# Rope: the cosine product from PSUM into a tile of its own

## The chip, the cores and the metric

The kernel runs on one core of one Trainium2 chip. A core has five engines that matter here: TensorE (PE) multiplies matrices into PSUM, VectorE (DVE) and ScalarE (ACT) work on SBUF and PSUM, GpSimd (POOL) works on SBUF, and SyncE (SP) issues the DMAs. Each engine runs its own list of instructions in order and waits on semaphores. The metric is the device time of one execution in microseconds (us), lower is better; a kernel's time is the median of its runs.

## The reference

One hybrid decoder block on a sequence of 1024 tokens of width 1024: an RMS norm, one wide projection, a forgetting attention (eight heads of 64) beside a differential attention (four heads with two 64-wide query and key parts each), SiLU gates, a merge by sigmoid gates, an output projection and a residual. Rope is applied to the queries and keys of the differential branch alone:

```python
def apply_rope(x, cos, sin):
    x1, x2 = jnp.split(x, 2, axis=-1)
    return jnp.concatenate([x1 * c - x2 * s, x2 * c + x1 * s], axis=-1)

qd = apply_rope(qb.reshape(b, s, DIFF_HEADS, 2, DIFF_QK_DIM).transpose(0, 2, 3, 1, 4), cos, sin)
kd = apply_rope(kb.reshape(b, s, DIFF_HEADS, 2, DIFF_QK_DIM).transpose(0, 2, 3, 1, 4), cos, sin)
...
out = (softmax(q1 k1^T) - lam * softmax(q2 k2^T)) v      # causal, per head
```

## The kernel before

The data are fp32. For the multiplications, operands are split into a high part (rounded to the type fp32r) and a low part (the rest), and a product is made of two or three such multiplications.

The kernel has three stages in time. First (to about 110 us) it loads and norms x, transposes it into `hT`, and projects the values (L195). Then (110 to about 555 us) comes the attention: eight units, `u` = 0 to 3 for the differential heads and 4 to 7 for pairs of forgetting heads. Last come the gates, the branch products and the output projection, which PE fills on its own.

In the attention stage, `unit_proj(u)` makes the transposed queries and keys of a unit in four tasks: `k` and `q`, each in two chunks of 512 tokens. A task loads and splits the weights once per kind (`load_w`, L264 on POOL and L266 on DVE), runs 24 matmuls into a PSUM tile of the tag `pj` (`project`, L276), and then, for differential units, calls `rope`; for forgetting units the PSUM tile goes on as it is. `stack` (L325 to L328) then splits the result into high and low halves, two ACT casts and two DVE subtractions. `pj` has two banks, shared with the other projections.

`rope` works on 128 rows: four blocks of 32, and the partner of a row lies in the neighbouring block. ACT copies the PSUM tile to SBUF (`raw`, L313). Four DMAs of 32 rows each (L317) write the blocks in exchanged order into `sw`. DVE multiplies `raw` by the cosines in place (L318), POOL multiplies `sw` by the signed sines (L319), DVE adds the two (L320). The DMAs read `raw`, and L318 overwrites it, so L318 waits for the four DMAs to have landed. There are 16 ropes: four units times q and k times two chunks.

The tiles of the tag `raw` come from three slots. The slots are shared with the spilled projections of `z` (`spill_tasks`, L369 to L371: ACT copy and a DMA to memory) and with the sums of squares of finished heads (`sum_squares`, L378 to L388).

The attention of a unit (`unit_attn`) goes row block by row block: scores into PSUM tiles of the tag `S` (three banks, L429 and L430), a DVE pass that adds the mask, writes the scores to SBUF and finds the row's extreme (L431), exp on ACT (L437), the normalization (L523 to L527), the transposes on PE (L458), their split by ACT (L461) and DVE (L462), and the product with the values (L482). While unit `u` is in its attention, the projections of unit `u + 1` and of `z` are called in between as filler (the loop at L651 to L663), and unit 0 projects before any attention (L627 to L629).

The order of instructions on each engine is not the order of the calls: a planner places them, by the order of the calls as priority and by its own costs of instructions and transfers, and it adds the waits. An engine then runs its list as planned, also when a transfer takes longer than the planner thought.

Of the kernel before, what the change touches and what calls it, by code (L numbers as in the profile page):

```python
# [9 lines left out]
F32 = mybir.dt.float32  # L10
F32R = mybir.dt.float32r
AF = mybir.ActivationFunctionType
ALU = mybir.AluOpType
# [3 lines left out]
P = 128  # L17
# [4 lines left out]
CH = 512  # L22
# [25 lines left out]
def tile_hybrid_block(  # L48
# [18 lines left out]
    nc = tc.nc  # L67
# [187 lines left out]
    def load_w(name, src, hi_act=False, lo_pool=False, pieces=None):  # L255
        raw = wpool.tile([P, KT, P], F32, tag="wraw", name=f"raw_{name}")
        for ks, piece in pieces or [(slice(0, KT), src)]:
            nc.sync.dma_start(raw[:, ks], piece)
        hi = wpool.tile([P, KT, P], F32R, tag="whi", name=f"hi_{name}")
        lo = wpool.tile([P, KT, P], F32R, tag="wlo", name=f"lo_{name}")  # L260
        if hi_act:
            nc.scalar.copy(hi, raw)
        else:
            nc.gpsimd.tensor_scalar(hi, raw, 1.0, 1.0, op0=ALU.mult, op1=ALU.mult)  # L264
        eng = nc.gpsimd if lo_pool else nc.vector
        eng.tensor_tensor(lo, raw, hi, op=ALU.subtract)  # L266
        return hi, lo

    def w_cols(c0):
        return w[:, c0:c0 + P].rearrange("(k p) n -> p k n", p=P)  # L270

    def project(ps, wt, c):
        hi, lo = wt
        for k in range(KT):
            for a, h in ((hi, 0), (hi, 1), (lo, 0)):
                nc.tensor.matmul(  # L276
                    ps, lhsT=a[:, k, :], rhs=hT[h][k // 4][c][:, k % 4, :],
                    start=(k == 0 and a is hi and h == 0), stop=(k == KT - 1 and a is lo))


    with ExitStack() as st:
# [3 lines left out]
        stg = st.enter_context(tc.tile_pool(name="stg", bufs=2, side="right", reuse_waits="tile"))  # L285
# [7 lines left out]
        cosT = big.tile([P, S], F32, tag="big", name="cosT")  # L293
# [7 lines left out]
        def unit_proj(u):  # L301

            diff = u < 4
            t = u if diff else u - 4
            qc, kc = (QB, KB_) if diff else (QA, KA_)
            T = {}
            for n in ("TA", "TB", "KA", "KB"):
                T[n] = qk.tile([P, S], F32R, tag=n, name=f"{n}{u}")

            def rope(ps, c, nm):  # L310
                sl = slice(c * CH, (c + 1) * CH)
                raw = stg.tile([P, CH], F32, tag="raw", name=f"raw{nm}", bufs=3)
                nc.scalar.copy(raw, ps)  # L313
                sw = stg.tile([P, CH], F32, tag="sw", name=f"sw{nm}")
                for b in range(4):
                    o = b ^ 1
                    nc.sync.dma_start(sw[b * 32:(b + 1) * 32, :], raw[o * 32:(o + 1) * 32, :])  # L317
                nc.vector.tensor_tensor(raw, raw, cosT[:, sl], op=ALU.mult)  # L318
                nc.gpsimd.tensor_tensor(sw, sw, sinT[:, sl], op=ALU.mult)  # L319
                nc.vector.tensor_tensor(raw, raw, sw, op=ALU.add)  # L320
                return raw

            def stack(A, B, src, sl):

                nc.scalar.copy(A[UPR, sl], src[UPR])  # L325
                nc.vector.tensor_tensor(A[DNR, sl], src[UPR], A[UPR, sl], op=ALU.subtract)
                nc.scalar.copy(B[DNR, sl], src[DNR])
                nc.vector.tensor_tensor(B[UPR, sl], src[DNR], B[DNR, sl], op=ALU.subtract)  # L328

            def q_chunk(wt, c):  # L330
                sl = slice(c * CH, (c + 1) * CH)
                ps = pj.tile([P, CH], F32, tag="pj", name=f"pq{u}_{c}")
                project(ps, wt, c)
                src = rope(ps, c, f"q{u}_{c}") if diff else ps
                stack(T["TA"], T["TB"], src, sl)

            def k_chunk(wt, c):
                sl = slice(c * CH, (c + 1) * CH)
                ps = pj.tile([P, CH], F32, tag="pj", name=f"pk{u}_{c}")
                project(ps, wt, c)  # L340
                src = rope(ps, c, f"k{u}_{c}") if diff else ps
                stack(T["KA"], T["KB"], src, sl)

            box = {}

            def mk(kind, c, c0):
                def run():
                    if kind not in box:
                        box[kind] = load_w(f"{kind}{u}", w_cols(c0))
                    (q_chunk if kind == "q" else k_chunk)(box[kind], c)  # L350
                return run

            tasks = [mk("k", 0, kc + t * P), mk("q", 0, qc + t * P),
                     mk("k", 1, kc + t * P), mk("q", 1, qc + t * P)]
            return T, tasks
# [4 lines left out]
        def spill_tasks(nm, c0, dst):  # L360
            box = {}

            def mk(c):
                def run():
                    if not box:
                        box[0] = load_w(nm, w_cols(c0))
                    ps = pj.tile([P, CH], F32, tag="pj", name=f"p{nm}_{c}")
                    project(ps, box[0], c)
                    zs = stg.tile([P, CH], F32, tag="raw", name=f"s{nm}_{c}", bufs=3)  # L369
                    nc.scalar.copy(zs, ps)  # L370
                    nc.sync.dma_start(dst[:, c * CH:(c + 1) * CH], zs)  # L371
                return run
            return [mk(0), mk(1)]

        def sum_squares(t, c):

            sl = slice(c * CH, (c + 1) * CH)
            sq = stg.tile([P, CH], F32, tag="raw", name=f"sq{t}_{c}", bufs=3)  # L378
            nc.sync.dma_start(sq, y_d[t][:, sl])
            nc.scalar.activation(sq, sq, AF.Square)  # L380
            hi, lo = (stg.tile([P, CH], F32R, tag="sw", name=f"sq{part}{t}_{c}") for part in range(2))
            nc.scalar.copy(hi, sq)
            nc.gpsimd.tensor_tensor(lo, sq, hi, op=ALU.subtract)
            ps = pj.tile([P, CH], F32, tag="pj", name=f"ssq{t}_{c}")[0:32]
            nc.tensor.matmul(ps, lhsT=onesr, rhs=hi, start=True, stop=False)
            nc.tensor.matmul(ps, lhsT=onesr, rhs=lo, start=False, stop=True)
            nc.scalar.copy(sq[0:1], ps[0:1])  # L387
            nc.sync.dma_start(ss_d[t:t + 1, sl], sq[0:1])  # L388
# [243 lines left out]
        for u in range(8):  # L632
# [13 lines left out]
            for t in SFILL[u]:  # L646
                fill += [lambda t=t, c=c: sum_squares(t, c) for c in range(2)]
                fill.append(lambda t=t: subln_scales(t))
# [397 lines left out]
```

## Time and profile before

| | us |
|---|---|
| three runs | 931.85, 937.65, 935.04 |
| median | 935.04 |
| the profiled execution | 932.72 |
| its span, first to last instruction | 930.9 |

| engine | busy us | share of the span |
|---|---|---|
| PE | 890.3 | 96% |
| VectorE (DVE) | 612.8 | 66% |
| GpSimd (POOL) | 483.3 | 52% |
| ScalarE (ACT) | 436.5 | 47% |

A row of the instructions in order of time reads: start, duration, engine, line, operation, output<-inputs, shapes and count, and in brackets the idle time of that engine just before and what ended it. A row of waits reads: engine and what it started, then what released it, total us, times, longest us. A row of groups ends with busy us and mean ns, then idle us before. `rawk` and `rawq` are the tiles of rope for k and q, `pk`, `pq` and `pz` the projections, `Sd` and `mxd` the scores and extremes of the differential heads, `ptd` and `pld` their transposes and low halves, `ypd` the product with the values.

### The profile page before, as it was taken

The page shows a single profiled execution, that of the slowest core. Times are in us where ns is not written, and L with a number is a line of the kernel's source. Part 1 is how long each engine was busy: PE and PEld are TensorE (multiplying, and loading weights), DVE is VectorE, ACT ScalarE, POOL GpSimd, SP SyncE. Part 2 cuts the span into 40 slices and gives each one's busy share as a digit, 9 for nine tenths or more (in the row PEclk, how much of TensorE's full clock was granted, in tenths as well). Part 3 has the DMA queues.
Part 4 walks back from the last instruction along what each step waited for, and adds up shares of the span by engine and source line. Part 5 has one row for each costly group of instructions (what it writes and reads, how often), then busy time and mean ns, then how long its engine had stood idle before and what let it go on. Part 6 is the DMA issues. An engine that isn't in the chain of part 4 may idle for free. (4 is left out here: it accounts for less than half of the span.)

```text
span 930.9 us, 13688 instructions
## 1 busy us (share of the span) xinstructions
PE 890.3 (96%) x4600; PEld 746.7 (80%) x4600; DVE 612.8 (66%) x1121; ACT 436.5 (47%) x861; POOL 483.3 (52%) x456
## 2 busy tenths in 40 slices
PE   7999999989999999999999999999999999999994
PEld 5899977767887888888888887788888888887873
DVE  6766566878678665557657547416768883549876
ACT  3433225556665675365555647523434450323331
POOL 7224334545555556254344446417677336878962
PEclk9999999999999999999999999999999999999998
DMA  9557646423526261432523432595655596211242
GB/s 317 187 179 269 245 110 177 108 69 90 140 53 191 53 180 39 136 85 76 159 71 82 133 102 59 210 399 193 211 170 168 159 360 226 69 46 46 91 136 91
DMA packets 118408, 136.95 MB, mean 147 GB/s; under 512 B 10289, under 2 KB 84017, under 8 KB 117314
## 3 DMA queue, kind: packets, MB, share of 16 engines
q1 hardware_dynamic: 118194, 135.82, 46.4%
q8 instruction: 36, 0.59, 0.3%
q14 instruction: 34, 0.28, 0.1%
q10 hardware_dynamic: 144, 0.26, 0.1%
HBM read 85.65 MB, written 37.81 MB: 133 GB/s over the span
## 5 line engine op out<-in xcount | busy, mean ns | idle before, releaser
L195 PE MATMUL pv<-wvhi,hT 128*128 128x264 f32 (+2 forms) x384 | 89.1, 324 | 0.4 <-DVE hT L181 0.4
L276 PE MATMUL pz<-hT,hi_z 128*128 128x512 f32 x256 | 83.9, 398 | 0.2 <-ACT sq L387 0.2
L276 PE MATMUL pq<-hT,hi_q 128*128 128x512 f32 x256 | 83.1, 394 | 0.0
L276 PE MATMUL pk<-hT,hi_k 128*128 128x512 f32 x256 | 81.3, 394 | 0.0
L732 PE MATMUL x_o<-wo_op,a_o 128*128 128x512 f32 x336 | 78.5, 393 | 2.9 <-POOL a_o L684 1.9
L866 PE MATMUL pb<-yT,hi_br 128*128 128x512 f32 x256 | 78.4, 389 | 0.0
L732 PE MATMUL x_g<-T,a_g 128*128 128x512 f32 x336 | 78.3, 392 | 0.0
L732 PEld LDWEIGHTS x_o<-wo_op,a_o 128*128 128x128 f32 x336 | 62.8, 188 | 18.4 <-POOL a_o L684 2.7
L732 PEld LDWEIGHTS x_g<-T,a_g 128*128 128x128 f32 x336 | 63.1, 188 | 14.1
L524 POOL TENSOR_SCALAR Pd<-Pd,l,nlam 128x128 f32<-128x128 f32 (+7 forms) x32 | 31.7, 992 | 77.6 <-DVE l L523 75.3
L437 ACT ACTIVATE Pd<-Pd,mxd 128x1024 f32<-128x1024 f32 (+7 forms) x64 | 49.8, 779 | 46.3 <-DVE mxd L431 44.4
L195 PEld LDWEIGHTS pv<-wvhi,hT 128*128 128x128 f32 x384 | 64.5, 190 | 6.1 <-DVE hT L181 0.7
L550 POOL TENSOR_TENSOR cb<-cb,trim 128x128 f32<-128x128 f32 x64 | 30.3, 478 | 67.8 <-DVE mxf L431 44.8
L555 POOL TENSOR_SCALAR Pf<-Pf,lf 128x1024 f32<-128x1024 f32 (+3 forms) x64 | 48.0, 754 | 27.9 <-DVE lf L554 24.8
L195 PE MATMUL pv<-wvlo,hT 128*128 128x512 f32 (+2 forms) x192 | 62.2, 326 | 0.0
L462 DVE TENSOR_TENSOR plf<-ptf,phf 128x512 fp32r<-128x512 f32 (+1 forms) x80 | 50.0, 635 | 18.4 <-ACT phf L461 17.6
L437 ACT ACTIVATE Pf<-Pf,mxf 128x1024 f32<-128x1024 f32 (+3 forms) x64 | 49.9, 779 | 20.9 <-DVE mxf L431 20.3
L732 PE MATMUL x_g<-hT,a_g 128*128 128x512 f32 x252 | 59.1, 392 | 0.0
L866 PEld LDWEIGHTS pb<-yT,hi_br 128*128 128x128 f32 x256 | 48.1, 188 | 9.9
L732 PEld LDWEIGHTS x_g<-hT,a_g 128*128 128x128 f32 x252 | 47.3, 188 | 10.5
L276 PEld LDWEIGHTS pk<-hT,hi_k 128*128 128x128 f32 x256 | 47.4, 188 | 9.6 <-DVE KB L328 0.6
L276 PEld LDWEIGHTS pq<-hT,hi_q 128*128 128x128 f32 x256 | 47.7, 188 | 9.2
(249 smaller groups left out, 2399.4 us busy)
## 6 DMA issues: line engine op xcount, KB each, us to landing
t_d<-t SPq DMA_DIRECT2D x16, 512.0 KB, 4.7
T<-t_d SPq DMA_DIRECT2D x8, 1024.0 KB, 17.7
raw<-in_w_in_dram SPq DMA_DIRECT2D x14, 512.0 KB, 3.9
vb_d<-vbs SPq DMA_DIRECT2D x8, 512.0 KB, 3.8
va_d<-vas SPq DMA_DIRECT2D x8, 512.0 KB, 3.0
raw_k<-in_w_in_dram SPq DMA_DIRECT2D x8, 512.0 KB, 4.2
raw_q<-in_w_in_dram SPq DMA_DIRECT2D x8, 512.0 KB, 4.5
V<-vb_d SPq DMA_DIRECT2D x4, 1024.0 KB
```

The source lines that it names most:

```text
L195: nc.tensor.matmul(ps[n], lhsT=hT[hp][k // 4][i // 4][:, k % 4, hs], rhs=wt[k][:, a:b], start=first, stop=(k == KT - 1 and hp == 1))
L276: nc.tensor.matmul(ps, lhsT=a[:, k, :], rhs=hT[h][k // 4][c][:, k % 4, :], start=(k == 0 and a is hi and h == 0), stop=(k == KT - 1 and a ...
L437: nc.scalar.activation(pr[:, 0:n], pr[:, 0:n], AF.Exp, bias=mx[:, len(pcs) - 1:len(pcs)], scale=-1.0, accum_out=le)
L462: nc.vector.tensor_tensor(pl[:, 0:n], pt[:, 0:n], ph[:, 0:n], op=ALU.subtract)
L524: nc.gpsimd.tensor_scalar(p2[:, 0:n], p2[:, 0:n], l2, nlam, op0=ALU.mult, op1=ALU.mult)
L550: nc.gpsimd.tensor_tensor(diag, diag, trim, op=ALU.add)
L555: nc.gpsimd.tensor_scalar(p1[:, 0:n], p1[:, 0:n], l1, 1.0, op0=ALU.mult, op1=ALU.mult)
L732: nc.tensor.matmul(x[m], lhsT=a[:, ai, k, :], rhs=right[m][bi][k], start=(k == 0 and n == 0), stop=(k == 3 and n == 2))
L866: nc.tensor.matmul(ps, lhsT=a[:, kk, :], rhs=yT[g][h][:, k % 2, sl], start=(k == 0 and a is hi and h == 0), stop=(k == 3 and a is lo))
```

## The change

The cosine product no longer works in place. It reads the projection a second time, straight from PSUM, and writes a new tile `rot` of the same tag `raw`; the sum with `sw` is made in `rot`, which goes on to `stack`. The copy of ACT is read by the four DMAs alone. The tag has four slots instead of three, everywhere that it is used; a rope now takes two of them. Lines after L317 move down by one in the changed kernel.

```diff
             def rope(ps, c, nm):
                 sl = slice(c * CH, (c + 1) * CH)
-                raw = stg.tile([P, CH], F32, tag="raw", name=f"raw{nm}", bufs=3)
+                raw = stg.tile([P, CH], F32, tag="raw", name=f"raw{nm}", bufs=4)
                 nc.scalar.copy(raw, ps)
                 sw = stg.tile([P, CH], F32, tag="sw", name=f"sw{nm}")
                 for b in range(4):
                     o = b ^ 1
                     nc.sync.dma_start(sw[b * 32:(b + 1) * 32, :], raw[o * 32:(o + 1) * 32, :])
-                nc.vector.tensor_tensor(raw, raw, cosT[:, sl], op=ALU.mult)
+                rot = stg.tile([P, CH], F32, tag="raw", name=f"rot{nm}", bufs=4)
+                nc.vector.tensor_tensor(rot, ps, cosT[:, sl], op=ALU.mult)
                 nc.gpsimd.tensor_tensor(sw, sw, sinT[:, sl], op=ALU.mult)
-                nc.vector.tensor_tensor(raw, raw, sw, op=ALU.add)
-                return raw
+                nc.vector.tensor_tensor(rot, rot, sw, op=ALU.add)
+                return rot
...
-                    zs = stg.tile([P, CH], F32, tag="raw", name=f"s{nm}_{c}", bufs=3)
+                    zs = stg.tile([P, CH], F32, tag="raw", name=f"s{nm}_{c}", bufs=4)
...
-            sq = stg.tile([P, CH], F32, tag="raw", name=f"sq{t}_{c}", bufs=3)
+            sq = stg.tile([P, CH], F32, tag="raw", name=f"sq{t}_{c}", bufs=4)
```

## The prediction

> **What bounds the kernel now.** I read the page's busy table and slices first, then a table of the stages around the rope, then the waits of the stage that holds the rope, then single instructions in order of time.
>
> ```profile
> span 930.9 us, 13688 instructions
> PE 890.3 (96%) x4600; PEld 746.7 (80%) x4600; DVE 612.8 (66%) x1121; ACT 436.5 (47%) x861; POOL 483.3 (52%) x456
> PE   7999999989999999999999999999999999999994
> PEclk9999999999999999999999999999999999999998
> ```
>
> TensorE (PE) is busy for 890.3 of 930.9 us, at its granted clock, in nearly every slice. The change removes no PE instruction, so all that it can win is PE idle time. The stages say where that lies (the columns are the stretch, its length, then busy time and count of PE, weight loads, VectorE, ScalarE and GpSimd):
>
> ```profile
> 110.00:137.00 27.00, 25.03 (x114) 20.52 (x113) 13.42 (x21) 5.41 (x10) 8.34 (x6) 1.00 0.41 114
> 137.00:300.00 163.00, 153.51 (x800) 126.82 (x799) 125.24 (x259) 95.11 (x196) 85.00 (x69) 1.00 0.47 123
> 300.00:550.00 250.00, 246.51 (x1396) 211.79 (x1395) 150.97 (x394) 146.30 (x311) 116.81 (x145) 1.00 0.36 102
> ```
>
> All 16 ropes lie between 110 and 300 us: three cosine products (L318) in the first stretch, thirteen in the second. PE idles 27.00 - 25.03 = 2.0 us in the first and 163.00 - 153.51 = 9.5 us in the second. That 9.5 us, 1.0% of the run, is a bound on the direct gain. The waits of 137 to 300 us (who waited for whom, total, times, longest) name the releasers:
>
> ```profile
> PE Sd L429 <- DVE mxd L431: 5.7, 8, 1.1
> PE ypd L482 <- DVE pld L462: 2.6, 4, 1.5
> DVE rawq L318 <- DMA swq<-rawq: 8.7, 4, 3.6
> DVE rawk L318 <- DMA swk<-rawk: 2.5, 2, 1.3
> DVE rawq L320 <- POOL swq L319: 3.8, 3, 1.8
> ```
>
> VectorE (DVE) releases 5.7 + 2.6 = 8.3 us of PE's 9.5: PE needs the score banks that L431 empties, and the low halves of L462. DVE itself stands still for 8.7 + 2.5 = 11.2 us in front of L318, six times, because L318 overwrites the tile that four DMAs are still reading. What counts is how much of the 11.2 reaches the 8.3. The longest of the six shows that it need not:
>
> ```profile
> 236.15 0.69 DVE L318 TENSOR_TENSOR rawq<-rawq,cosT 128x512 f32<-128x512 f32 x1 [3.61 <-DMA swq<-rawq]
> 234.47 0.71 PE L276 MATMUL pz<-hT,hi_z 128*128 128x512 f32 x2
> 238.21 0.28 PE L429 MATMUL Sd<-KB,TB 128*128 128x256 f32 x1
> ```
>
> DVE stands from 232.5 to 236.15, and PE runs the projection of z (L276) through it; no PE row there has an idle time in front. PE has filler work, and a DVE stall costs only where it leaves a backlog that lasts until PE comes back to the scores.
>
> **The change part by part.** PE: nothing added. ScalarE (ACT): the same copy (L313). SyncE: the same four DMAs per rope, from the same tile, at the same place in its queue. GpSimd (POOL): the same sine product (L319). DVE: the same number of operations; L318 loses its wait for the DMAs, reads PSUM for its first input, and writes another tile. L320 still waits for POOL and so, behind it, for the DMAs.
>
> First term, the duration of L318 and of what runs beside it: single rows, and two groups of the same subtraction (L326), once with its input in SBUF and once in PSUM:
>
> ```profile
> 166.91 0.69 DVE L318 TENSOR_TENSOR rawk<-rawk,cosT 128x512 f32<-128x512 f32 x1 [1.15 <-DMA swk<-rawk]
> 221.53 1.19 DVE L318 TENSOR_TENSOR rawk<-rawk,cosT 128x512 f32<-128x512 f32 x1
> 166.95 1.80 POOL L319 TENSOR_TENSOR swk<-swk,sinT 128x512 f32<-128x512 f32 x1
> 220.66 1.51 POOL L319 TENSOR_TENSOR swk<-swk,sinT 128x512 f32<-128x512 f32 x1 [0.20 <-DMA swk<-rawk]
> 157.01 1.29 POOL L319 TENSOR_TENSOR swq<-swq,sinT 128x512 f32<-128x512 f32 x1
> L326 DVE TENSOR_TENSOR KA<-rawk,KA 64x512 fp32r<-64x512 f32 x7 | 7.2, 1034 | 1.7 <-ACT KA L325 1.6
> L326 DVE TENSOR_TENSOR KA<-pk,KA 64x512 fp32r<-64x512 f32 x8 | 5.5, 684 | 3.4 <-ACT KA L325 3.2
> ```
>
> L318 and L319 are released by the same DMAs and lengthen one another: L319 takes 1.80 beside the L318 of 166.91 and 1.29 alone, and the L318 of 221.53, which starts while an L319 runs, takes 1.19. With the input in PSUM, the L326 group takes 684 ns where the SBUF form takes 1034. I take 0.69 for every new L318. That returns 1.19 - 0.69 = 0.5 us of DVE at 221.53, and 1.80 - 1.29 = 0.5 us of POOL at 166.95. The Trainium skill (SBUF — State Buffer, section Who interferes with whom) says that a DVE operation with two SBUF inputs contends with a GpSimd operation that reads SBUF, and one with a single SBUF input does not. The trace agrees (1034 against 684 ns). By that rule the return at 221.53 is sure; without it, the sum below would be 0.5 us smaller.
>
> Second term, the stalls. After the change DVE does L318 before the DMAs land, and the stall, if any is left, stands in front of L320, behind whatever the planner puts between the two. I look at which PE idle follows a stall or a lengthened L318 with DVE full in between:
>
> ```profile
> 167.52 0.68 DVE L431 CUSTOM_DVE_ANT_0 Pd<-Sd,dmask 128x512 f32<-128x512 f32 x1
> 168.79 0.69 DVE L320 TENSOR_TENSOR rawk<-rawk,swk 128x512 f32<-128x512 f32 x1 [0.49 <-POOL swk L319]
> 172.29 0.50 PE L429 MATMUL Sd<-KA,TA 128*128 128x512 f32 x1 [0.42 <-DVE mxd L431]
> 176.69 0.44 PE L429 MATMUL Sd<-KA,TA 128*128 128x384 f32 x1 [1.14 <-DVE mxd L431]
> 182.37 0.50 PE L429 MATMUL Sd<-KA,TA 128*128 128x512 f32 x1 [0.63 <-DVE mxd L431]
> 225.22 0.39 PE L482 MATMUL ypd<-pld,V 128*128 128x256 f32 x1 [0.66 <-DVE pld L462]
> 228.49 0.39 PE L429 MATMUL Sd<-KB,TB 128*128 128x256 f32 x1 [1.06 <-DVE mxd L431]
> ```
>
> The first three PE waits (0.42 + 1.14 + 0.63 = 2.2 us) come after the stall of 1.15 us at 166.91. With L318 done ahead of it, the score work that stood behind L318 also moves ahead, so DVE comes out earlier by at most that stall, 1.15, and by no less than the 0.5 that POOL's L319 gains; I take 1.1, as L318 itself (0.69) and the L431 at 167.52 (0.68) can fill the stall. The last two PE waits (1.7 us) follow the lengthened L318 at 221.53, so 0.5 of them goes. The others do not hang on L318:
>
> ```profile
> 158.33 1.49 DVE L320 TENSOR_TENSOR rawq<-rawq,swq 128x512 f32<-128x512 f32 x1 [1.84 <-POOL swq L319]
> 160.48 0.44 PE L429 MATMUL Sd<-KB,TB 128*128 128x384 f32 x1 [0.73 <-DVE mxd L431]
> 203.53 0.38 PE L482 MATMUL ypd<-pld,V 128*128 128x256 f32 x1 [1.50 <-DVE pld L462]
> ```
>
> At 160.48 PE waits behind an L320 that waits for POOL, whose L319 ran alone (1.29); at 203.53 behind the sums of the forget gate. Gain on PE: 1.1 + 0.5 = 1.6 us. The ends are nothing at all and 8.3.
>
> Third term, the opening, where four ropes follow one another with no attention beside them:
>
> ```profile
> 116.45 0.59 ACT L313 COPY rawk<-pk 128x512 f32<-128x512 f32 x1 [1.73 <-PE pk L276]
> 117.56 1.22 DVE L266 TENSOR_TENSOR lo_q<-raw_q,hi_q 128x1024 fp32r<-128x1024 f32 x1 [2.41 <-DMA va_d<-vas]
> 118.83 0.50 PE L276 MATMUL pq<-hT,lo_q 128*128 128x512 f32 x1 [1.97 <-DVE lo_q L266]
> 124.34 0.69 DVE L318 TENSOR_TENSOR rawk<-rawk,cosT 128x512 f32<-128x512 f32 x1 [5.56 <-DMA swk<-rawk]
> ```
>
> The first L318 stood 5.56 us and PE lost nothing by it. After the change it can start when the copy ends, 116.45 + 0.59 = 117.04, and end at 117.73, which pushes L266 from 117.56 by 0.2 us; PE waits for that L266. If the planner puts it behind L266 the cost is nil. I charge 0.2.
>
> Fourth term, the PSUM bank. It is now free after the copy; afterwards it is free after copy and L318. Two banks take turns, and one projection is the cover:
>
> ```profile
> 123.95 0.62 PE L276 MATMUL pk<-hT,hi_k 128*128 128x512 f32 x2
> 129.39 0.62 PE L276 MATMUL pq<-hT,hi_q 128*128 128x512 f32 x2
> 300.25 0.56 ACT L325 CAST KA<-pk 64x512 fp32r<-64x512 f32 x1
> 305.78 0.69 DVE L328 TENSOR_TENSOR KB<-pk,KB 64x512 fp32r<-64x512 f32 x1
> ```
>
> A projection takes at least 129.39 - 123.95 = 5.4 us. The units without rope already hold a bank from 300.25 to 306.47, 6.2 us, and PE idles only 250.00 - 246.51 = 3.5 us in all of 300 to 550. I take nothing for this term; without that cover each microsecond by which L318 ends more than 5.4 us after the projection is a microsecond of PE. The Trainium skill (PSUM — Partial Sum Buffer, section PSUM bank collisions raise a hardware error) says that two engines may not read one bank at once, two readers included, and speaks against the change: L318 then cannot run beside the copy but waits for its end. No run here shows such a pair. By it the hold is 0.59 + 0.69 = 1.3 us instead of 0.69, still inside 5.4, so the sum is the same either way.
>
> Fifth term, the slots. A rope takes two of four instead of one of three: the copy's until its DMAs land, the product's until its last subtraction (L328). In the opening the copies are some 5.4 us apart, and each slot comes free before the next copy needs it; nothing charged.
>
> Sum: -1.1 - 0.5 + 0.2 = -1.4 us. The profiled execution took 932.72 us (span 930.9 and 1.8 around it), so 931.3 is its answer; the median of the three runs, 935.04, is 2.3 above that execution, and I forecast 935.0 - 1.4 = 933.6.
>
> **The rivals.** A, the wait only changes its name, chance 0.22: the planner may leave L318 and L320 side by side, so DVE stands before L320 for as long as it stood before L318. For it: already now it waits there 3.8 us (the row of rawq), and L320 needs the same DMAs. Against it: after 166.91 it put score work (L431) between. Time 935.
>
> B, the stage clears, chance 0.16: DVE's 11.2 us of stalls vanish, the backlog with them, and PE loses none of the 8.3 us. For it: PE's idle time is DVE's doing almost alone. Against it: half of it follows other work, as shown. Time 935.0 - 8.3 = 926.7, and if the stages behind also shift, a little less.
>
> C, slower, chance 0.14: L318 becomes a wait at the head of DVE's queue for PE and ACT. DVE runs in order; what stands behind L318 is L431, and PE's scores wait for L431's banks. It decides when DVE arrives at L318 before the copy has ended, or late enough (5.4 us) to hold the bank against PE. For it: DVE is busy 125.24 of 163.00 us, so it is often late. Against it: the six-microsecond holds from 300 us on. Price: one more PE wait of the kind seen, 5.7 / 8 = 0.7 us, for each of thirteen ropes, 9.3 us: 944.3, and more where slots run out too.
>
> **How the numbers follow.** My forecast has 0.48, and lies between 930 and 936. About 1% is what a measurement of this kernel can tell from no change: below 925.7 or above 944.4. B lies at that edge and gives 0.10 to faster and 0.06 to same; C gives 0.11 to slower and 0.03 to same; all else is same: 0.10, 0.79, 0.11. The range takes in B's 926.7 and most of the way to C: 926 to 943.
>
> **What would show it.** Right: every cosine product at 0.69 us; no DVE wait for the swap's DMAs, and more wait of the addition for POOL, but less than 11.2 + 3.8 us; sine products nearer 1.29; PE idle in 137 to 300 us near 8 of 163. Wrong: PE waiting in front of a projection for a cosine product (C by the bank), DVE waiting at it for PE or ACT (C by the queue), or a PE idle time that falls by 5 us or more (B).

## The result and the profile after

The changed kernel takes 922.89 us (median of four runs, 922.54 to 923.97), the kernel before 935.25 (four runs, 931.85 to 937.65). The ratio is 0.9881, with a 95% interval from 0.9858 to 0.9904: 12.4 us or 1.2% faster. The forecast was 933.6 with a range from 926 to 943, so the result lies outside the range, on the fast side. The profiled execution after took 923.97 us, the slowest of its four; the one before took 932.72, under its median. The two profiles lie 8.7 us apart and can show no more of the gain than that.

First the page after, its span and busy times:

```profile
span 922.2 us, 13691 instructions
PE 887.2 (96%) x4600; PEld 746.7 (81%) x4600; DVE 604.9 (66%) x1121; ACT 436.3 (47%) x861; POOL 477.0 (52%) x456
```

The counts of instructions are the same, and DVE and POOL lost 7.9 and 6.3 us of busy time. The same stretches as in the prediction, after the change:

```profile
110.00:137.00 27.00, 24.49 (x115) 20.21 (x115) 11.54 (x21) 5.30 (x10) 5.83 (x5) 1.00 0.41 115
137.00:300.00 163.00, 159.09 (x844) 133.69 (x843) 124.35 (x281) 104.26 (x215) 86.62 (x74) 1.00 0.47 126
300.00:550.00 250.00, 247.87 (x1407) 213.81 (x1406) 148.77 (x388) 142.08 (x303) 113.23 (x145) 1.00 0.36 103
```

PE's idle time in 137 to 300 us fell from 9.5 to 163.00 - 159.09 = 3.9 us. The cosine and sine products of all ropes, in groups, first of the kernel before and then of the changed one:

```profile
L318 DVE TENSOR_TENSOR rawk<-rawk,cosT 128x512 f32<-128x512 f32 x8 | 8.1, 1014 | 8.1 <-DMA swk<-rawk 8.0
L318 DVE TENSOR_TENSOR rawq<-rawq,cosT 128x512 f32<-128x512 f32 x8 | 6.5, 814 | 8.8 <-DMA swq<-rawq 8.7
L319 POOL TENSOR_TENSOR swq<-swq,sinT 128x512 f32<-128x512 f32 x8 | 12.8, 1606 | 12.3 <-DMA swq<-rawq 12.3
```

```profile
L319 DVE TENSOR_TENSOR rotq<-pq,cosT 128x512 f32<-128x512 f32 x8 | 5.5, 684 | 0.6 <-ACT rawq L313 0.6
L319 DVE TENSOR_TENSOR rotk<-pk,cosT 128x512 f32<-128x512 f32 x8 | 5.5, 684 | 0.3 <-ACT rawk L313 0.3
L320 POOL TENSOR_TENSOR swq<-swq,sinT 128x512 f32<-128x512 f32 x8 | 10.4, 1295 | 15.0 <-DMA swq<-rawq 15.0
```

All sixteen cosine products now take 0.68 to 0.69 us, 3.6 us less in sum, and DVE waits for the copy only 0.9 us in all. So the products did what the prediction said. The DVE waits of the rope, 137 to 300 us, did not go away. Before, two rows of the addition at L320 and two of the product at L318 make 8.7 + 2.5 + 3.8 + 1.7 = 16.7 us (three of them stand in the prediction). This is the fourth:

```profile
DVE rawk L320 <- POOL swk L319: 1.7, 2, 1.2
```

After, with the addition at L321:

```profile
DVE rotk L321 <- POOL swk L320: 8.6, 5, 3.9
DVE rotq L321 <- POOL swq L320: 6.3, 4, 2.8
DVE rotq L319 <- ACT rawq L313: 0.6, 1, 0.6
DVE rotk L319 <- ACT rawk L313: 0.3, 1, 0.3
```

8.6 + 6.3 + 0.6 + 0.3 = 15.8 us. The wait has changed its name, as rival A says, and yet the kernel is faster. What PE saved must be found on PE.

**Where the time went.** The differential attention reaches from the first score matmul of the tile `Sd` to the first of `Sf`, 137.10 to 346.20 us before and 138.80 to 337.60 after: 209.1 and 198.8 us, 10.3 less. The stretch behind it, to the end, takes 584.7 and 584.6. The stage itself begins 1.7 us later, so that 8.7 us are left between the two profiles. Over all profiles of this study it begins between 136.2 and 139.9 us, in no order by the rope, and I do not read the 1.7 as an effect. I cut the stage into four parts at the same score rows of both kernels: the ninth of unit 0, the first of unit 1, the third of unit 1. Before (columns as in the prediction):

```profile
137.10:172.29 35.19, 33.10 (x158) 26.68 (x156) 24.48 (x55) 18.44 (x41) 18.66 (x17) 1.00 0.67 174
172.29:193.53 21.24, 18.55 (x89) 14.50 (x89) 17.68 (x28) 10.53 (x20) 9.55 (x7) 1.00 0.31 80
193.53:211.85 18.32, 16.31 (x88) 13.14 (x89) 15.45 (x29) 11.00 (x20) 5.68 (x4) 1.00 0.30 76
211.85:346.20 134.35, 129.98 (x712) 109.93 (x712) 97.98 (x230) 87.48 (x184) 75.25 (x62) 1.00 0.44 119
```

After:

```profile
138.80:173.55 34.75, 32.66 (x161) 26.82 (x159) 27.36 (x57) 19.04 (x43) 18.17 (x16) 1.00 0.65 173
173.55:189.84 16.29, 16.27 (x85) 13.40 (x86) 12.59 (x30) 10.87 (x19) 8.98 (x7) 1.00 0.38 105
189.84:203.73 13.89, 13.43 (x75) 11.10 (x74) 9.97 (x26) 9.28 (x19) 5.49 (x5) 1.00 0.32 81
203.73:337.60 133.87, 132.19 (x727) 112.86 (x726) 95.94 (x229) 88.66 (x185) 71.14 (x62) 1.00 0.44 120
```

Parts 2 and 3 are 4.95 and 4.4 us shorter. But part 4 has 15 matmuls more and parts 2 and 3 have 17 fewer: some filler moved from the one to the other, so lengths alone mislead. The waits mislead less, if they are read from the right rows. A score matmul of the kernel before stands in the prediction with a wait of 1.14 us, at 176.69. The load of its weights starts at the same moment and shows more:

```profile
176.69 0.19 PEld L429 LDWEIGHTS Sd<-KA,TA 128*128 128x128 f32 x1 [1.57 <-DVE mxd L431]
```

The end of a matmul's row is modelled: the matmuls in front of this one start 0.23 us apart and are drawn 0.39 us long, so the idle time behind the last of them comes out short. Neither row is exact. The matmul before starts at 175.16, which makes this one 176.69 - 175.16 - 0.23 = 1.30 us late. The waits of the weight loads over the stage, before:

```profile
PEld Sd L429 <- DVE mxd L431: 11.3, 14, 1.6
PEld ypd L482 <- DVE pld L462: 4.6, 6, 1.9
PEld ypd L482 <- ACT phd L461: 1.9, 3, 0.7
PEld ptd L458 <- POOL Pd L527: 1.4, 3, 0.9
```

And after:

```profile
PEld Sd L430 <- DVE mxd L432: 6.9, 13, 1.5
PEld pk L276 <- DVE KB L329: 1.1, 1, 1.1
PEld ptd L459 <- POOL Pd L528: 1.0, 2, 0.8
PEld pz L276 <- DVE rotq L319: 0.3, 1, 0.3
```

With the rows not shown, each of 0.3 us or less, they sum to 20.1 and 9.3 us. 209.1 - 20.1 = 189.0 and 198.8 - 9.3 = 189.5: the stage is some 189 us of TensorE work and its waits, before and after. The change took 10.8 us of waits away. By matmul rows PE's idle time in the stage fell from 11.2 to 4.2 us, or by 6.9, which is not enough for the 10.3. By the four parts the weight loads waited 3.7, 4.2, 3.3 and 8.9 us before, and 3.0, 1.0, 0.9 and 4.5 after: 0.7, 3.2, 2.4 and 4.4 us less.

In part 2 the rows of DVE show what moved. Before, part 2 begins with the low half of unit 2's key weights and the last subtraction of unit 1's keys. Only behind them comes the score pass that frees the bank for the matmul at 176.69:

```profile
172.15 2.06 DVE L266 TENSOR_TENSOR lo_k<-raw_k,hi_k 128x1024 fp32r<-128x1024 f32 x1
174.24 1.67 DVE L328 TENSOR_TENSOR KB<-rawk,KB 64x512 fp32r<-64x512 f32 x1
175.94 0.69 DVE L431 CUSTOM_DVE_ANT_0 Pd<-Sd,dmask 128x512 f32<-128x512 f32 x1
```

After, both run ahead of part 2, which begins at 173.55:

```profile
169.76 1.23 DVE L266 TENSOR_TENSOR lo_k<-raw_k,hi_k 128x1024 fp32r<-128x1024 f32 x1
171.02 1.95 DVE L329 TENSOR_TENSOR KB<-rotk,KB 64x512 fp32r<-64x512 f32 x1
```

DVE's busy time in part 2 fell from 17.68 to 12.59 us, and in part 1 it rose from 24.48 to 27.36.

### The profile page after: what moved, and what is told of

Its sections match the earlier page's. It is cut to its first block, busy times and chain, and to the rows that moved or that the text cites. A ratio compares the mean times of both kernels' runs of the same rounds, so it can differ in the third digit from the quotient of the medians.

```text
span 922.2 us, 13691 instructions
## 1 busy us (share of the span) xinstructions
PE 887.2 (96%) x4600; PEld 746.7 (81%) x4600; DVE 604.9 (66%) x1121; ACT 436.3 (47%) x861; POOL 477.0 (52%) x456
## 5 line engine op out<-in xcount | busy, mean ns | idle before, releaser
L438 ACT ACTIVATE Pd<-Pd,mxd 128x128 f32<-128x128 f32 (+7 forms) x64 | 49.6, 775 | 35.5 <-DVE mxd L432 35.1
L525 POOL TENSOR_SCALAR Pd<-Pd,l,nlam 128x128 f32<-128x128 f32 (+7 forms) x32 | 29.3, 917 | 66.5 <-DVE l L524 60.3
L733 PEld LDWEIGHTS x_g<-hT,a_g 128*128 128x128 f32 x252 | 47.3, 188 | 10.5
```

Source lines behind the costliest of these rows:

```text
L438: nc.scalar.activation(pr[:, 0:n], pr[:, 0:n], AF.Exp, bias=mx[:, len(pcs) - 1:len(pcs)], scale=-1.0, accum_out=le)
L525: nc.gpsimd.tensor_scalar(p2[:, 0:n], p2[:, 0:n], l2, nlam, op0=ALU.mult, op1=ALU.mult)
L733: nc.tensor.matmul(x[m], lhsT=a[:, ai, k, :], rhs=right[m][bi][k], start=(k == 0 and n == 0), stop=(k == 3 and n == 2))
```

## The experiments

Four theories came up one after the other. T1, the stall: DVE no longer stands in front of the product for the four DMAs, and the score work behind it runs sooner. T2, the port: the product and its neighbours on POOL no longer lengthen one another, and DVE has time back. T3, the accident: the forget gate's sums, or some other unrelated work, collide in the old plan and not in the new. T4, the weights: the split of unit 2's query weights stands in front of the last scores of unit 0 in the old plan and behind them in the new. All kernels below were timed in five rounds beside the kernel before, whose median was 933.5 to 934.7 us; against these the changed kernel gains 10.6 to 11.8 us. Stage lengths and waits are those of each one's profiled execution; the verdicts go by the medians.

**The change in pieces.** e2 reads PSUM, but works in place, and so keeps the wait:

```diff
-                nc.vector.tensor_tensor(raw, raw, cosT[:, sl], op=ALU.mult)
+                nc.vector.tensor_tensor(raw, ps, cosT[:, sl], op=ALU.mult)
```

> One half of the change: the cosine product reads PSUM but still overwrites the copy in place, so it still waits for the four DMAs; three slots as before. If the gain is the wait for the DMAs that VectorE no longer stands in (theory 1), this kernel stays within 3 us of the kernel before (932 to 938), with VectorE still waiting some 11 us for the DMAs in front of the product. If the gain is the contention of the product with GpSimd (theory 2), it takes most of the 12 us: 923 to 927, products all at 0.69 us and sine products near 1.29 us.

e3 has the tile of its own and the four slots, but reads SBUF:

```diff
+                rot = stg.tile([P, CH], F32, tag="raw", name=f"rot{nm}", bufs=4)
+                nc.vector.tensor_tensor(rot, raw, cosT[:, sl], op=ALU.mult)
...
+                nc.vector.tensor_tensor(rot, rot, sw, op=ALU.add)
```

> The other half: the product has its own tile and no longer waits for the DMAs, but reads the copy in SBUF; four slots, the PSUM bank free after the copy as before. Theory 1 (the wait): 922 to 927. Theory 2 (contention): 930 to 936, with products up to 1.8 us. If both are needed, between, about 929.

e4 is the changed kernel with three slots (`bufs=3` at all four places):

> The changed kernel with three staging slots instead of four. If the fourth slot carries part of the gain, or three are too few for two tiles per rope, the time rises by 3 us or more above 923; if the slots play no part, 922 to 924. The planned order of VectorE is the same as with four.

e8 is the changed kernel with the addition on POOL, so that DVE no longer waits in front of it:

```diff
-                nc.vector.tensor_tensor(rot, rot, sw, op=ALU.add)
+                nc.gpsimd.tensor_tensor(rot, rot, sw, op=ALU.add)
```

> The changed kernel with the addition of the rope moved from VectorE to GpSimd, behind the sine product. VectorE then never stands in front of the addition (in the changed kernel 8.6 + 6.3 = 14.9 us from 137 to 300 us). If such stalls are what PE pays for (theory 1), a further gain of 2 to 5 us: 918 to 921. If what is left of PE's idle time has other causes, 922 to 925; if GpSimd becomes late by its additional 1.3 us per rope, 926 or more.

| kernel | median us | ratio to before, 95% | stage, weight-load waits (us) |
|---|---|---|---|
| changed | 922.89 | 0.9881 (0.9858 to 0.9904) | 198.8, 9.3 |
| e2, PSUM in place | 924.89 | 0.9903 (0.9882 to 0.9924) | 203.0, 7.4 |
| e3, own tile, SBUF | 926.59 | 0.9922 (0.9905 to 0.9939) | 202.0, 11.8 |
| e4, three slots | 922.69 | 0.9883 (0.9862 to 0.9904) | 201.1, 12.4 |
| e8, addition on POOL | 923.64 | 0.9885 (0.9866 to 0.9904) | 197.2, 7.8 |

The stages of e2 and the kernel before do not hold the same work: 1071 matmuls against 1045, by filler that the plan moved. Lengths are to be compared only where the counts agree.

e2 still has the wait, in 137 to 300 us (its lines are those of the kernel before):

```profile
DVE rawk L318 <- DMA swk<-rawk: 7.6, 4, 4.2
DVE rawq L318 <- DMA swq<-rawq: 2.8, 3, 1.9
```

It stands for 10.4 us where the kernel before stood for 11.2, and is 9.2 us faster than its own before of 934.12. So T1 as a sum of stalls is not the cause: the sum can stay, and most of the gain comes. But in e2 the stalls stand at other ropes. The one that the prediction names, 1.15 us in front of the third product of unit 1 (166.91), is gone in e2 as it is in the changed kernel, so e2 does not clear that one. e2 also pays for its stalls in a way of its own: the product that waits for the DMAs holds its PSUM bank, and PE's next projections wait for it, 3.3 us in the stage by matmul rows:

```profile
PE pz L276 <- DVE rawk L318: 2.3, 1, 2.3
PE pq L276 <- DVE rawq L318: 1.0, 1, 1.0
```

e8 was meant to show the other side. In its list of DVE waits in 137 to 300 us no line names the exchange or the sine product any more, only 1.9 us for the copy, and the time is that of the changed kernel. But the stall has only moved once more: the casts of `stack` on ACT wait for the addition on POOL, and DVE waits for the casts, where the changed kernel has 1.0 and 1.3 us:

```profile
DVE TA L327 <- ACT TA L326: 8.1, 6, 2.1
DVE KA L327 <- ACT KA L326: 7.3, 4, 4.7
```

So e8 is no test of a DVE without stalls. The fourth slot is worth nothing that can be measured (e4). But e3 gains 7.5 us with the product still in SBUF, and with one product that still takes 2.58 us, so T2 alone falls too. The intervals of e3 and e4 just miss one another, 0.9905 against 0.9904 at their near ends, and the medians are 3.9 us apart: that much the PSUM read may be worth on top of e3. Of the 11.4 us of e4, e2 brings 9.2 and e3 7.5: either half of the change brings about two thirds or more, and the two do not add.

**The sums of the forget gate.** In the plan before, PE's longest wait in part 3, 1.94 us by the weight load at 203.53, follows this row of DVE and POOL:

```profile
199.02 4.41 DVE L611 TENSOR_SCALAR fs<-fg 128x64 f32<-128x64 f32 x1
200.67 2.76 DVE L608 RECIPROCAL fs<-fs 128x64 f32<-128x64 f32 x1
201.14 2.29 DVE L462 TENSOR_TENSOR pld<-ptd,phd 128x384 fp32r<-128x384 f32 x1
199.78 2.38 POOL L527 TENSOR_TENSOR Pd<-Pd,Pd 128x1024 f32<-128x1024 f32 x1
202.12 1.25 POOL L319 TENSOR_TENSOR swk<-swk,sinT 128x512 f32<-128x512 f32 x1
```

Three DVE operations all end at 203.43, just after POOL's train ends at 202.12 + 1.25 = 203.37. In the changed kernel the same two small operations meet no such train:

```profile
192.17 0.20 DVE L612 TENSOR_SCALAR fs<-fg 128x64 f32<-128x64 f32 x1
194.42 0.55 DVE L609 RECIPROCAL fs<-fs 128x64 f32<-128x64 f32 x1 [1.41 <-ACT fs L608]
```

T3 says that this is where the gain comes from. Three tests. f1 and f2 are the kernels before and after with the sums made early, ahead of unit 0's attention; n2 is the kernel before with an unrelated tile in four buffers, which shifts the plan just ahead of the sums:

```diff
+        forget_sums()
         pend = None
...
-            if u == 1:
-                forget_sums()
```

```diff
-            t = qk.tile([P, 2 * P], F32R, tag=f"X{m}", name=f"X{m}{nm}_{g}", bufs=3)
+            t = qk.tile([P, 2 * P], F32R, tag=f"X{m}", name=f"X{m}{nm}_{g}", bufs=4)
```

> The kernel before, rope untouched, with the sums of the forget gate computed ahead of unit 0's attention instead of at the start of unit 1. In the kernel before they fell at 195 to 204 us behind a train of GpSimd operations, and small VectorE operations of 0.2 us took 4.4 and 2.8 us there; in the changed kernel they took 0.2 and 0.55. Theory 3 (half of the gain is that this collision is gone, by a shift of the plan that the change happened to bring): 926 to 930, 5 to 8 us under the kernel before, without any change to rope. If the collision cost PE nothing (theories 1 and 2 alone): 932 to 937.

> The changed kernel with the same early sums. Theory 3: little is left to win, 920 to 924, so that against the other kernel with early sums the rope is worth some 5 us. If the collision played no part, the difference of the two kernels with early sums stays at 12 us. If it was all of it, the two agree within 2 us.

> The kernel before with a fourth buffer for the swapped queries of the scores (tags X0 and X1), which has nothing to do with rope; it moves the planned order of VectorE from the middle of unit 0's attention on, just ahead of the sums of the forget gate. If such a shift of the plan is enough to miss the collision (theory 3), 924 to 930. If the gain needs rope (theories 1 and 2), 932 to 937.

And f3 and f4 are the kernels before and after with the sums made later, at unit 3 (`if u == 3:`):

> The kernel before with the sums of the forget gate at the start of unit 3 instead of unit 1: a third plan with the old rope. If every plan with the old rope ends near 934 (as with the sums at unit 0 and at unit 1), 932 to 937; if the sums at unit 1 are the accident that costs the kernel before, 925 to 930.

> The changed kernel with the sums at the start of unit 3. If the worth of the new rope is that VectorE loses less time to the port that it shares with GpSimd, whatever the plan (theory 2), 8 to 12 us under the other kernel with late sums. If the size hangs on the plan (theory 3: 12 us in one plan, 3 us with early sums), anything between 2 and 12 us under it.

| sums of the forget gate | rope before | rope changed | gain us |
|---|---|---|---|
| at unit 1, as they are | 935.25 | 922.89 | 12.4 |
| late, at unit 3 (f3, f4) | 939.45 | 933.71 | 5.7 |
| early (f1, f2) | 934.58 | 931.56 | 3.0 |

As a sole cause T3 falls: taking the collision away in the kernel before gives nothing (f1: 1.0006, 0.9991 to 1.0021), since in its profile the waits come back elsewhere (part 3 falls from 3.3 to 0.8 us, part 1 rises from 3.7 to 6.6; 21.0 us in the four parts instead of 20.1). n2 measured 934.52, ratio 1.0001 (0.9985 to 1.0016), and says less: its shift did not miss the collision, L611 is held for 3.20 us there. f2 and f3 fell outside every range expected of them: early sums cost the changed kernel 8.7 us, and late sums cost the kernel before some 6 (f3: 1.0069, 1.0048 to 1.0089). But the size of the gain does hang on work that the change does not touch: the same edit is worth 12.4, 5.7 or 3.0 us.

**Which unit's ropes.** The changed rope for some units only, four slots everywhere (`if u < 2:`, `if u >= 2:`, `if u == 0:`, `if u == 1:` ahead of the changed body, else the old one):

```diff
+                if u == 1:
...
+                    nc.vector.tensor_tensor(rot, ps, cosT[:, sl], op=ALU.mult)
+                    nc.gpsimd.tensor_tensor(sw, sw, sinT[:, sl], op=ALU.mult)
+                    nc.vector.tensor_tensor(rot, rot, sw, op=ALU.add)
+                    return rot
```

> The new rope for units 0 and 1 alone, the old one for units 2 and 3; four slots. The two traces differ most from 150 to 212 us, while unit 0 attends and unit 1's ropes run: 923 to 926 if the gain lies there.

> The new rope for units 2 and 3 alone, four slots. If the gain lies with unit 1's ropes, 931 to 935; if every rope gives the same 0.7 us, 928 to 930.

> The new rope in unit 0 alone, that is in the four ropes ahead of any attention, where PE is full and never waits for a rope. If a gain needs PE idle time beside the rope: 932 to 936. If the opening hands a better plan or an earlier VectorE to unit 0's attention: 923 to 929.

> The new rope in unit 1 alone, whose ropes run as filler of unit 0's attention. If the gain of the first two units is made where PE waits: 922 to 927. If it comes from the opening: 931 to 935.

The four numbers of a row are the weight loads' waits in the four parts of the stage, as above:

| ropes changed | median us | ratio to its own runs of before, 95% | waits by part |
|---|---|---|---|
| none | 935.25 | | 3.7, 4.2, 3.3, 8.9 |
| unit 0 (q0) | 932.31 | 0.9989 (0.9975 to 1.0004) | 2.2, 4.2, 3.3, 8.6 |
| units 2, 3 (p2) | 934.18 | 1.0000 (0.9987 to 1.0014) | 3.4, 4.2, 3.3, 7.3 |
| unit 1 (q1) | 924.55 | 0.9901 (0.9881 to 0.9920) | 6.3, 1.0, 0.9, 4.3 |
| units 0, 1 (p1) | 922.60 | 0.9888 (0.9869 to 0.9908) | 2.5, 1.0, 0.9, 5.0 |
| all | 922.89 | 0.9881 (0.9858 to 0.9904) | 3.0, 1.0, 0.9, 4.5 |

Four ropes of sixteen, those of unit 1, bring nearly all of it. They run in parts 1 and 2, beside unit 0's attention. In q1 the ropes of units 2 and 3 are the old ones, and yet parts 3 and 4 lose 2.4 and 4.6 us of waits, while p2, which changes just those ropes, loses 1.6 in part 4 and nothing of the time. So the gain in part 2 belongs to unit 1's ropes, and the gain behind it follows from the same edit, with the old ropes there; through which steps of the plan is not shown. The fall in part 2 is the steadiest number of the study: from 4.2 to 1.0 us in none against all, q0 against q1, p2 against p1 and f3 against f4, and from 3.9 to 1.4 in f1 against f2. What varies is the rest: 6.8 us in parts 3 and 4 with the sums at unit 1, 2.2 with late sums (18.8 to 16.6), 1.8 with early sums (10.5 to 8.7).

Two things in DVE's rows go with the fall in part 2. The first is unit 1's third rope (166.91 before). In all eight profiles with the old rope in unit 1 (the kernel before, f1, f3, n2, p2, q0, r1, r2) DVE loses 1.5 to 2.4 us there, by a wait of the product, a product longer than 0.69 us or a wait of the addition. In the twelve others it loses nothing, but for 1.1 us in e3. The second is the pair of 172.15 and 174.24: it runs at or behind the ninth score row in all the eight and ahead of it in ten of the twelve. Neither is shown to be the cause. In k2, below, one of the pair runs at the ninth row and part 2 waits 2.7 us; in e2 both run behind it and part 2 waits 0.0.

**More load on POOL.** If T2 is the currency, work on POOL that reads SBUF should give the time back, and work that only writes should not, or less. k1 and k2 are e4 with added POOL work behind each rope's addition, into a tile that nothing reads: k1 a product of two tables, k2 two fills.

```diff
+                dump = stg.tile([P, CH], F32, tag="dump", name=f"dump{nm}", bufs=1)
+                nc.gpsimd.tensor_tensor(dump, sinT[:, sl], cosT[:, sl], op=ALU.mult)
```

```diff
+                for _ in range(2):
+                    nc.gpsimd.memset(dump, 0.0)
```

> The changed kernel (three slots) with one more GpSimd operation behind each addition, a product of the sine and cosine tables into a tile that nobody reads, some 1.29 us: a dose of GpSimd reading SBUF, 16 times. Theory 2 (VectorE loses time to the port shared with GpSimd): VectorE's busy time rises by 5 us or more and the time by 2 to 8 us, 925 to 931. If contention is not what PE pays for: 922 to 925.

> The control to it: two fills of the same tile with zeros instead, which occupy GpSimd about as long but read nothing. Theory 2: VectorE's busy time and the time stay within 2 us of the changed kernel, 921 to 925. If the longer GpSimd queue or the shifted plan is what costs, it rises as much as with the reading operation.

k1 took 927.86 us (0.9936, 0.9918 to 0.9953), k2 927.28 (0.9928, 0.9909 to 0.9947): 5.2 and 4.6 more than e4. The stage of e4, k1 and k2:

```profile
138.50:339.60 201.10, 195.39 (x1045) 164.07 (x1044) 147.34 (x340) 128.75 (x266) 104.93 (x89) 1.00 0.47 126
136.90:341.60 204.70, 199.44 (x1058) 169.02 (x1059) 159.53 (x341) 130.15 (x268) 118.66 (x96) 0.98 0.46 124
136.80:341.00 204.20, 197.49 (x1053) 166.03 (x1053) 151.20 (x339) 128.87 (x266) 109.96 (x94) 1.00 0.46 124
```

DVE is busy 12.2 us longer in k1 and 3.9 in k2, and both cost about the same. So time that DVE loses beside POOL is no measure of what PE pays, and T2 in its simple form, so many microseconds of DVE for so many of the kernel, does not hold here. The test is blunt: the planner placed the work anew in both, the granted clock of k1's profiled stage was 0.98, and PE's weight-load waits in the stage did not grow (12.4 us in e4, 9.7 and 12.6 in k1 and k2), so it is not shown what the added work costs by.

**The weights of unit 2.** In the kernel before, the low half of unit 2's query weights keeps DVE from 187.43 (2.25 idle before it) to 192.81, ahead of the score pass at 192.72; after, it comes behind the last of them and has no wait:

```profile
189.68 3.13 DVE L266 TENSOR_TENSOR lo_q<-raw_q,hi_q 128x1024 fp32r<-128x1024 f32 x1 [2.25 <-POOL hi_q L264]
192.72 0.74 DVE L431 CUSTOM_DVE_ANT_0 Pd<-Sd,dmask,mxd 128x512 f32<-128x512 f32 x1
```

```profile
189.51 1.23 DVE L266 TENSOR_TENSOR lo_q<-raw_q,hi_q 128x1024 fp32r<-128x1024 f32 x1
```

That is T4. r1 is the kernel before with this one low half on POOL, r2 with this one high half on ACT; r3 is the changed kernel with the high half on ACT, as a control.

```diff
-                        box[kind] = load_w(f"{kind}{u}", w_cols(c0))
+                        box[kind] = load_w(f"{kind}{u}", w_cols(c0), False, u == 2 and kind == "q")
```

```diff
-                        box[kind] = load_w(f"{kind}{u}", w_cols(c0))
+                        box[kind] = load_w(f"{kind}{u}", w_cols(c0), u == 2 and kind == "q", False)
```

> The kernel before, old rope, with one VectorE operation less: the low half of unit 2's query weights (L266, at 189.68 us in the kernel before) is made on GpSimd. In the kernel before that operation stood 2.25 us for GpSimd and then took 3.13 us, ahead of the last score rows of unit 0; in the changed kernel it comes behind them. Theory 4 (the new rope moves unit 2's weight split out of the way of unit 0's last scores): the stretch from the ninth score row of unit 0 to unit 1's first falls from 21.2 to 16 to 18 us and the time by 3 to 6 us, 928 to 931. If that operation only filled time: 932 to 936.

> The kernel before, old rope, with the high half of the same weights made by ScalarE instead of GpSimd, so that the low half on VectorE has not to wait for GpSimd; the planned order of VectorE differs in two places only. Theory 4: 2 to 4 us under the kernel before, 930 to 932. If the wait is replaced by another: 933 to 936.

> The control: the same edit in the changed kernel, with the order of VectorE and PE unchanged. Theory 4: nothing is left to win there, 921 to 924. If it gains as much as in the kernel before, the edit's gain has nothing to do with what the rope change did: 918 to 920.

r1 took 931.94 us (0.9979, 0.9963 to 0.9995), r2 933.20 (0.9995, 0.9978 to 1.0012), r3 922.19 (0.9879, 0.9855 to 0.9903). The kernel before of these runs had 933.47. r1 gains 1.5 us, and its wait in part 2 falls from 4.2 to 3.2, not to 1.0. In r2 the wait only found another releaser:

```profile
188.71 2.45 DVE L266 TENSOR_TENSOR lo_q<-raw_q,hi_q 128x1024 fp32r<-128x1024 f32 x1 [2.05 <-ACT hi_q L262]
```

So T4 is worth some 1.5 us of the 12.4, and 3.5 at most by the interval of r1. No kernel of the study beats the changed one by more than can be measured: e4, p1 and r3 lie at 922.2 to 922.7.

**What stays open.** Every edit makes the planner order DVE anew, and I could not take a wait or a collision away and hold the order. It is shown where the gain is made (unit 1's ropes), on what rows (weight loads that wait for DVE) and that its size hangs on the plan around it. It is not shown why each half of the change alone, the PSUM read or the tile of its own, leads part 2 to nearly the same end (waits of 0.0 in e2, 1.3 in e3, 1.0 in the changed kernel).

## Why the prediction was wrong, step by step

**The bound was read from the wrong rows.** The prediction took 8.3 us of waits from PE's matmul rows in 137 to 300 us as the far end of the gain. The weight loads in the whole stage show 11.3 + 4.6 = 15.9 us for the same two releasers and 20.1 in all, and the stage goes on to 346 us. This step failed: the second term and rival B were both sized against a bound of about half of that, and the stage alone got 10.3 us shorter, more than the 9.5 that the prediction called a bound. The range's low end of 926 was rival B rounded down, so the result fell below it.

**Second term, the stall at 166.91: 1.1 us.** The step named the score rows at 172.29, 176.69 and 182.37. Their weight loads, with the one of 179.97 between, wait 0.84 + 1.57 + 0.55 + 1.06 = 4.0 us before. After, the ninth row alone waits 1.45 and three others 0.18, 0.26 and 0.24, 2.1 in all. So 1.9 us were won where 1.1 was said: right place, too small. The reason given, the stall that goes, is neither shown nor ruled out, since this stall is gone in e2 too. The limit put on it, that DVE comes out earlier by at most 1.15 us, did not hold: DVE had 5.1 us less to do in part 2, because other operations were placed ahead of it.

**First and second term, the lengthened product at 221.53: 0.5 us of two waits.** The first term counted one lengthened product of four. Those at 129.02, 134.75 and 258.74 took 1.67, 1.68 and 1.78 us, and the sixteen products together gave back 3.6. The waits at 225.22 and 228.49 are 0.90 and 1.50 us by the weight loads, and both are gone or small after (the nearest is 0.31 at 226.19). They also go in q1, where this rope is not changed: no row there waits for DVE between 211 and 250 us. So the size was wrong by a factor of four, and the rope at 221.53 need not change for them to go.

**"The others do not hang on L318".** This is the step that failed most. 160.48 and 203.53 were set aside because of what stands before them in the old plan, and the prediction took the plan behind the edit as given. The wait of 1.94 us at 203.53 went when the plan moved by a few microseconds, the 1.01 at 193.53 too, and parts 3 and 4 together lost 6.8 us of waits, against 3.9 in parts 1 and 2. In q1 they lost 7.0, with the old ropes in both. The prediction says that an engine follows its list; it did not ask how far the list changes.

**Third term, the opening: +0.2 us.** PE's wait for L266 grew from 2.4 to 2.9 us by the weight loads, so the direction was right and the size 0.5. q0, with unit 0's ropes alone, has no measurable gain.

**Fourth and fifth terms, bank and slots: nothing.** Right for this kernel. PE waits for a cosine product in front of a projection once, 0.3 us (the last of the rows after, above). DVE waits for the copy 0.9 us in the stage, so the two readers of one bank do go one after the other, and it costs PE no more than that. The condition that the prediction put on it, a product in time, matters: in e2 the product at 222.02 stands 4.20 us for its DMAs, and PE's next projection waits 2.3 us for it. Four slots against three: e4.

**The rivals.** A is right in its mechanism, 16.7 against 15.8 us, and wrong in its time, because the sum of DVE's waits is not what PE pays for. B comes nearest in its time, 926.7, and by the prediction's own mark (PE's idle time falls by 5 us or more; it fell by 5.6), but DVE's stalls did not vanish, and no kernel here is without them. Against B the prediction said that half of the 8.3 us follows other work, as shown; the two rows shown for it make 0.73 + 1.50 = 2.2. C did not occur in the changed kernel; its wait by the bank shows in e2.

**What was right.** The products at 0.69 us, no DVE wait for the exchange in front of them, sine products of q at 1.30 instead of 1.61, the costless bank and slots.

## What to carry to other kernels

Where TensorE bounds the kernel and a planner writes the order, size what an edit may win by TensorE's weight-load waits over the whole stage, not by matmul rows, and let the range reach to all of it: an edit in one place may take away waits that have nothing to do with it. A gain of this kind belongs to the edit and to the plan together, so measure the edit in two or three plans (here 12.4, 5.7 and 3.0 us) before its mechanism is believed. Applying it to one unit at a time found the four ropes that mattered in four kernels. And before a kernel is called free of a stall, look where the waiting went: in e8 it stood in another place.

## What the runs showed of the hardware

A DVE operation on 128x64 that takes 0.20 us alone was held for 4.41 us, from 199.02 until POOL's back-to-back instructions ended at 203.37; it did not get in between them, and the operations behind it on DVE ended with it. The Trainium skill (SBUF — State Buffer, section Who interferes with whom) says that a `tensor_scalar` can enter a mode that takes the port pair shared with GpSimd, and that who holds it blocks the other for the whole instruction. The trace agrees that it was blocked; which mode the operation ran in, it does not show. Here the hold went on over three POOL instructions. The changed kernel has a second case: L602 on 128x64 takes 1.37 us from 189.03 and ends at 190.40, just after POOL's fill (L617) at 190.34.

POOL work that only writes (k2) also went with more DVE time, 3.9 us against 12.2 for work that reads, though the plan differs.

Two kernels whose DVE order is the same, the changed one and e4, have profiled executions that differ in part 1 of the stage by 2.7 us (34.75 and 37.43) and by 3.5 us of weight-load waits (3.0 and 6.5), while parts 2 and 3 agree to 0.1 us; their medians agree to 0.2. The profiled execution of e4 took 925.37 us, 2.7 above its own median. One profiled execution carries that much chance, so the waits of a part are read here as an effect only where they repeat over several kernels, as those of part 2 do.
